# Giving two of GpSimd's one-operation instructions a second operation (a multiplication by one)

## The chip, the core and the metric

The kernel runs on one core of one Trainium2 chip. The metric is the device time of one execution in microseconds. Engines are called as the profile calls them: PE is TensorE's matmul, PEld its weight load, DVE is VectorE, ACT is ScalarE, POOL is GpSimd, SP is SyncE, which here only issues transfers.

## The reference

One layer of an encoder over 1024 positions of width 1024, all in float32. Cut to what this change touches:

```python
def rmsnorm(x, w):
    y = x * lax.rsqrt(jnp.mean(x * x, axis=-1, keepdims=True) + EPS)
    return y * w
...
h = rmsnorm(x, norm_mix_w) * (1 + sc_m) + sh_m
z, xbc, dt_raw, q, k, v = jnp.split(h @ w_in, IN_SPLITS, axis=-1)
y_ssd = ssd_mixer(z, xbc, dt_raw, ...)            # a scan over chunks, with an rmsnorm at its end
# attention: 8 heads of 64, each chunk of 64 positions sees itself and 8 chunks before it
scores = einsum(q, k) * 64 ** -0.5
p = softmax(where(valid, scores + bias, min), axis=-1)
y_att = einsum(p, v)
x = x + g_m * (concat([y_ssd, y_att]) @ w_out)
x = x + g_f * conv_ffn(rmsnorm(x, norm_ffn_w) * (1 + sc_f) + sh_f)
return rmsnorm(x, final_norm_w)
```

## The kernel before

**Stages.** The kernel first norms x and multiplies it into the first two pairs of heads' q, k and v (0 to about 102 us in the trace), then does attention (about 102 to 312 us, mingled with the projections that come next), the scan and the projection to x (to about 600 us), and the feed-forward part (from there to the end). Float32 products are made from a high and a low part, three matmuls for one (lines 76 to 78); `split` makes the two parts (lines 85 and 86).

**Attention.** The eight heads go in four pairs `p`, each pair in four units `u`, each unit in two rows of 128 queries (`i` = 2u and 2u + 1) and two heads `h`. `attn_scores` does one `i`: PE writes scores of up to 640 keys into PSUM (line 262); DVE adds the bias, negates and takes the minimum over the row (line 413); ACT takes the exponential and the row sum (line 416); DVE inverts the sum (line 418); POOL scales the row in place by it (line 419, one operand a column of one number per partition). The tile is `p`, of which there are eight buffers. `attn_pv` then transposes each scaled tile in blocks of 128 on PE, ACT and DVE split the result, and PE multiplies it with v:

```python
                if c0 == 0:
                    T.transpose(tps[:, o:o + P], p0[:, (j - lo0) * P:(j - lo0 + 1) * P], ident)   # line 445
                ...
                    T.transpose(tps[:, o1:o1 + P], p1[:, (j - lo1) * P:(j - lo1 + 1) * P], ident) # line 448
            split(hi, lo, tps[:, 0:used], A, V)
            ...
                T.matmul(pv[:, c0:c0 + n], w, hi[:, o:o + n], start=g == 0, stop=False)           # line 456
```

Between the units stand other products: the q, k and v of the later pairs (`gemm_part`, into PSUM tiles named `acc`), and beside the last pair the first projection of the scan (tiles named `s`, lines 76 to 78). For PE they are filling: they need nothing from attention. POOL also makes the low part of some weights there (line 86, `wl`), and blanks two corners of each bias tile (lines 475 and 476).

**The norms.** `rstd` takes a mean of squares, adds epsilon on POOL (line 116) and raises it to the power of minus one half on POOL (line 117). It runs 16 times on one column: 8 times in the first stage, 8 times in the scan. The norms at the end use another function (line 931), which the change leaves alone.

**What sets the order.** Nothing in these stages is ordered by hand but for a few places. The framework schedules the whole program when it is built: it reckons a duration for each instruction, and by these sets the order of instructions on every engine and of transfers on SP's queue. Each engine then runs its own list in that order, so an instruction that is not ready holds up all behind it on its engine. A change of one instruction's reckoned duration can so move instructions on every engine.

Of the kernel before, what the change touches and what calls it, by code (L numbers as in the profile page):

```python
# [13 lines left out]
ALU = mybir.AluOpType  # L14
# [50 lines left out]
def tile_block(ctx: ExitStack, tc: tile.TileContext, x, crep, pk, w_ada, w_first, w_ft, w_z,  # L65
# [3 lines left out]
    G = nc.gpsimd  # L69
# [36 lines left out]
    def stat(n=1):  # L106
        if stc[0] + n > 64:
            stc[0] = 0
        a = st1[:, stc[0]:stc[0] + n]
        stc[0] += n  # L110
        return a

    def rstd(ms, eps=EPS):
        n = ms.shape[-1]
        r = stat(n)
        G.tensor_scalar(ms, ms, eps, None, op0=ALU.add)
        G.tensor_tensor(r, ms, mhalf[:, 0:n], ALU.pow)
        return r

# [132 lines left out]
    def scores(p, i):  # L252
        d = qk[p]
        j0 = max(0, i - 4)
        n = (i - j0 + 1) * P
        off = (j0 - (i - 4)) * P
        parts = [(0, n)] if n <= 512 else [(0, 320), (320, 320)]
        st = [s_tile(), s_tile()]
        for h in range(2):
            for pi, (a, w) in enumerate(parts):  # L260
                for ti, kn in enumerate(("kh", "kl")):
                    T.matmul(st[h][:, 512 * pi:512 * pi + w], d["q"][h][:, i * P:(i + 1) * P],
                             d[kn][h][:, j0 * P + a:j0 * P + a + w], start=ti == 0, stop=ti == 1)
        return st, n, off, parts
# [31 lines left out]
    def norm1(st):  # L296
        ms = stat()
        junk = s0.tile([P, D], F32, tag="junk", name="junk")
        norm_to(xts[st], junk, ms)
        r = rstd(ms)  # L300
        V.tensor_scalar(xts[st], xts[st], r, None, op0=ALU.mult)
# [93 lines left out]
    def p_tile():  # L395
        return pp.tile([P, 640], F32, tag="p", name="p")
# [4 lines left out]
    def attn_scores(p, i, bt):  # L401
        st, n, off, parts = s00 if p + i == 0 else scores(p, i)
        res = []
        for h in range(2):
            pt_ = p_tile()
            nm, rs = stat(), stat()
            if len(parts) == 1:
                src, bsl, dst = st[h][:, 0:n], bt[h][:, off:off + n], pt_[:, 0:n]
            else:
                src = st[h].rearrange("p (a b) -> p a b", a=2)[:, :, 0:320]  # L410
                bsl = bt[h].rearrange("p (a b) -> p a b", a=2)
                dst = pt_.rearrange("p (a b) -> p a b", a=2)
            V.tensor_tensor_reduce(out=dst, in0=src, in1=bsl, scale=-1.0, scalar=3e38,  # L413
                                   op0=ALU.add, op1=ALU.min, accum_out=nm)
            pv_ = pt_[:, 0:n]
            A.activation(pv_, pv_, AF.Exp, scale=-1.0, bias=nm, accum_out=rs)
            rr = stat()
            last_v[:] = [V.reciprocal(rr, rs).ins]  # L418
            G.tensor_scalar(pv_, pv_, rr, None, op0=ALU.mult)  # L419
            res.append(pt_)  # L420
        return res

# [46 lines left out]
    def attention(p, extra=()):  # L469
        extra = dict(extra)  # L470
        bt = []
        for h in range(2):
            t = bp.tile([P, 640], F32, tag="bias", name="bias")
            nc.sync.dma_start(t, bias[2 * p + h])
            G.memset(t[0:64, 576:640], -1e30)
            G.memset(t[64:128, 0:64], -1e30)
            bt.append(t)
        for u in range(4):
            pa = attn_scores(p, 2 * u, bt)
            pb = attn_scores(p, 2 * u + 1, bt)  # L480
            for fn in extra.get(u, ()):
                fn()
            if p == 3:
                if u < 2:
                    early[4 + 2 * u] = wu_pair(w_ft[4 + 2 * u], A, G)
                for _ in range(MODS[u]):
                    mod_col(todo.pop(0), mtq[len(todo) % 4], last_v[0])
            for h in range(2):
                attn_pv(p, u, h, pa[h], pb[h])
# [345 lines left out]
    def ssd_norm(c, y, t, at=None):  # L835
        with tc.issue_after(at) if at else ExitStack():
            V.tensor_tensor(y, y, zs[:, c, 0:512], ALU.mult)
        ms = stat()
        A.activation(t, y, AF.Square, accum_out=ms)
        r = rstd(ms, 512.0 * EPS)  # L840
        A.activation(y, y, AF.Copy, scale=r)
# [724 lines left out]
```

## Time and profile before

| | us |
|---|---|
| median of 3 runs (1219.9 to 1223.88) | 1221.77 |
| the profiled execution | 1219.7 |
| its span, first to last instruction | 1217.7 |
| PE busy | 1167.9 |
| DVE busy | 927.8 |
| ACT busy | 597.0 |
| POOL busy | 199.9 |
| POOL's scaling, line 419, 64 instructions | 98.8 |
| POOL's epsilon, line 116, 16 instructions | 6.8 |

The mean clock granted to PE is 0.994. Busy PE is not PE at its peak, since matmuls overlap and their ends are modelled. Idle time of an engine is put down to what ended it. The numbers of the trace come from one execution, whose time outside the span is 2.0 us.

### The profile page before, as it was taken

How to read it: one execution, taken by the hardware profiler on the slowest of the kernel's cores; microseconds unless marked ns; L12 is line 12 of the kernel's file. 1: busy time of each engine (PE TensorE's matmuls, PEld its weight loads, DVE VectorE, ACT ScalarE, POOL GpSimd, SP SyncE). 2: the span in 40 equal slices, each digit the busy share in tenths (PEclk: the TensorE clock that was granted, in tenths of full speed). 3: DMA queues.
4: the chain of work that ended last, by engine and by line, in shares of the span. 5: the costliest groups of instructions: out<-in, count | busy, mean ns of one | idle time of the engine just before them, and what ended most of it. 6: DMA issues, size and time to landing. Idle time of an engine off the chain costs nothing.

```text
span 1217.7 us, 15636 instructions
## 1 busy us (share of the span) xinstructions
PE 1167.9 (96%) x5802; PEld 974.4 (80%) x5802; DVE 927.8 (76%) x1394; ACT 597.0 (49%) x1001; POOL 199.9 (16%) x174
## 2 busy tenths in 40 slices
PE   4998899989999989999999999999999999999996
PEld 3877787878878978888878888888888888888885
DVE  6846454686597678746999988988889869756986
ACT  4536454674243666676644533344334445433444
POOL 1205563672000034300000000000000000000522
PEclk9999999999999999999999999999999999999998
DMA  9722211311477201141123223322232278733443
GB/s 334 256 58 64 65 56 46 102 66 52 152 248 241 88 13 40 53 150 58 70 95 112 104 95 130 124 77 85 104 130 98 83 277 278 266 120 130 149 137 146
DMA packets 56395, 150.86 MB, mean 124 GB/s; under 512 B 5632, under 2 KB 5760, under 8 KB 54912
## 3 DMA queue, kind: packets, MB, share of 16 engines
q1 hardware_dynamic: 49264, 125.49, 30.6%
q10 hardware_dynamic: 7056, 24.38, 5.0%
q8 instruction: 45, 0.74, 0.3%
q14 instruction: 30, 0.25, 0.1%
HBM read 116.56 MB, written 29.10 MB: 120 GB/s over the span
## 4 chain that ended last, share of the span: by engine, by line
PE 80%; DVE 10%; ACT 4%; DMA 2%; issue 2%; POOL 1%; SPq 0%; POOLq 0%; DVEq 0%; ACTq 0%
PE wops L699 5%; PE dn L78 5%; PE dn L76 5%; PE dn L77 5%; PE uY L76 5%; PE uY L78 5%; PE uY L77 4%; PE uX L78 3%; PE uX L76 3%; PE uZ L77 3%; PE uX L77 3%; PE uZ L76 3%; PE uZ L78 3%; PE s L76 3%; PE s L77 2%; PE s L78 2%
## 5 line engine op out<-in xcount | busy, mean ns | idle before, releaser
L1427 POOL TENSOR_TENSOR ya<-ya,xs 128x512 f32<-128x512 f32 x4 | 17.2, 4334 | 557.7 <-ACT xs L1423 557.7
L77 PE MATMUL dn<-w 128*128 128x512 f32 x296 | 108.1, 392 | 0.0
L76 PE MATMUL dn<-w 128*128 128x512 f32 x296 | 108.1, 391 | 0.0
L419 POOL TENSOR_SCALAR p<-p,st 128x640 f32<-128x640 f32 (+4 forms) x64 | 98.8, 1558 | 43.9 <-DVE st L418 36.6
L78 PE MATMUL dn<-w 128*128 128x512 f32 x296 | 100.2, 391 | 0.2 <-DVE w L86 0.2
L76 PE MATMUL uY<-tH,w 128*128 128x512 f32 x248 | 97.2, 392 | 0.0
L77 PE MATMUL uY<-tL,w 128*128 128x512 f32 x248 | 97.0, 391 | 0.0
L78 PE MATMUL uY<-tH,w 128*128 128x512 f32 x248 | 96.9, 391 | 0.0
L85 ACT ACTIVATE w<-ya 128x1024 fp32r<-128x1024 f32 (+1 forms) x41 | 39.2, 956 | 87.5 <-PE uY L78 84.2
L699 PE MATMUL wops<-hH,yhl 128*128 128x512 f32 x224 | 74.1, 399 | 2.9 <-DVE yhl L86 1.5
L78 PEld LDWEIGHTS dn<-w 128*128 128x128 f32 x296 | 55.4, 188 | 13.3 <-DVE w L86 1.1
L76 PEld LDWEIGHTS dn<-w 128*128 128x128 f32 x296 | 55.5, 188 | 12.3
L77 PEld LDWEIGHTS dn<-w 128*128 128x128 f32 x296 | 55.5, 188 | 12.2
L85 ACT ACTIVATE w<-xs 128x1024 fp32r<-128x1024 f32 (+1 forms) x41 | 39.1, 954 | 37.3 <-PE uY L78 33.3
L78 PEld LDWEIGHTS uY<-tH,w 128*128 128x128 f32 x248 | 46.5, 188 | 10.4
L76 PEld LDWEIGHTS uY<-tH,w 128*128 128x128 f32 x248 | 46.6, 188 | 10.3
L77 PEld LDWEIGHTS uY<-tL,w 128*128 128x128 f32 x248 | 46.6, 188 | 10.2
L413 DVE CUSTOM_DVE_ANT_0 p<-s,bias 128x640 f32<-128x640 f32 (+4 forms) x64 | 40.4, 651 | 17.0 <-PE tp L445 5.2
L76 PE MATMUL s<-hH,wh 128*128 128x512 f32 x128 | 50.1, 391 | 2.4 <-DVE ct L520 2.3
L86 DVE TENSOR_TENSOR pt<-tp,pt 128x512 fp32r<-128x512 f32 (+2 forms) x72 | 41.5, 595 | 13.2 <-ACT pt L85 12.8
L699 PEld LDWEIGHTS wops<-hH,yhl 128*128 128x128 f32 x224 | 41.8, 188 | 12.2 <-DVE yhl L86 1.9
L1101 DVE SCALAR_TENSOR_TENSOR a<-cv,pkt,a 128x1023 f32<-128x1023 f32 (+1 forms) x40 | 51.1, 1279 | 0.1
(459 smaller groups left out, 3428.8 us busy)
## 6 DMA issues: line engine op xcount, KB each, us to landing
wos<-in_w_ada_dram SPq DMA_DIRECT2D x25, 512.0 KB, 4.6
gz<-a ACTq DMA_DIRECT2D x10, 1024.0 KB, 5.0
ya<-in_w_up_dram SPq DMA_DIRECT2D x11, 768.0 KB, 4.2
xs<-in_w_up_dram SPq DMA_DIRECT2D x11, 768.0 KB, 4.3
adat<-in_w_ada_dram SPq DMA_DIRECT2D x16, 512.0 KB, 5.5
raws<-in_w_ft_dram SPq DMA_DIRECT2D x14, 512.0 KB, 4.2
gy<-a ACTq DMA_DIRECT2D x10, 512.0 KB, 2.6
qk<-in_x_dram SPq DMA_DIRECT2D x8, 512.0 KB, 6.6
```

Source lines behind the costliest of these rows:

```text
L76: T.matmul(ps, lh, rh, start=start, stop=False, skip_group_check=more)
L77: T.matmul(ps, lh, rl, start=False, stop=False, skip_group_check=more)
L78: T.matmul(ps, ll, rh, start=False, stop=stop, skip_group_check=more)
L85: i = A.activation(hi, src, AF.Copy) if ehi is A else ehi.tensor_copy(hi, src)
L86: return i, elo.tensor_tensor(lo, src, f32(hi), ALU.subtract)
L413: V.tensor_tensor_reduce(out=dst, in0=src, in1=bsl, scale=-1.0, scalar=3e38, op0=ALU.add, op1=ALU.min, accum_out=nm)
L419: G.tensor_scalar(pv_, pv_, rr, None, op0=ALU.mult)
L699: i = op(*a, **k)
L1101: V.scalar_tensor_tensor(a[:, j:S], c[:, 0:S - j], w[2 - j], a[:, j:S], op0=ALU.mult, op1=ALU.add)
L1427: G.tensor_tensor(src, src, fnr[:, halves[1]], ALU.mult)
```

## The change

Both POOL instructions get a second operation, a multiplication by 1.0, in the same instruction. The values stay the same, and no instruction is added or removed.

```diff
     def rstd(ms, eps=EPS):
         n = ms.shape[-1]
         r = stat(n)
-        G.tensor_scalar(ms, ms, eps, None, op0=ALU.add)
+        G.tensor_scalar(ms, ms, eps, 1.0, op0=ALU.add, op1=ALU.mult)
         G.tensor_tensor(r, ms, mhalf[:, 0:n], ALU.pow)
         return r
...
             rr = stat()
             last_v[:] = [V.reciprocal(rr, rs).ins]
-            G.tensor_scalar(pv_, pv_, rr, None, op0=ALU.mult)
+            G.tensor_scalar(pv_, pv_, rr, 1.0, op0=ALU.mult, op1=ALU.mult)
             res.append(pt_)
```

It also moves instructions, since the scheduler reckons another duration for these two. Up to the start of attention all engines' lists are as before; from the first scaled tiles on PE's list differs in 39 places up to the scan, and is the same again after that.

The first place on PE is in pair 0, unit 0. `p_935` and `p_940` are the scaled tiles of the second row of queries, one for each head; `s_989` and `s_990` are scores of unit 1, `s_1055` of unit 2.

```order
 L262 MATMUL s_989<-qk_136,qk_134 128x512
 L262 MATMUL s_989<-qk_138,qk_134 128x512
+L448 MATMUL tp_946<-ident_69,p_935 128x128 x2
 L262 MATMUL s_990<-qk_137,qk_135 128x512
 L262 MATMUL s_990<-qk_139,qk_135 128x512
-L448 MATMUL tp_946<-ident_69,p_935 128x128 x2
+L448 MATMUL tp_960<-ident_69,p_940 128x128 x2
 L262 MATMUL s_1055<-qk_136,qk_134 128x320
 L262 MATMUL s_1055<-qk_138,qk_134 128x320
 L262 MATMUL s_1055<-qk_136,qk_134 128x320
 L262 MATMUL s_1055<-qk_138,qk_134 128x320
-L448 MATMUL tp_960<-ident_69,p_940 128x128 x2
```

The transposes of both scaled tiles now stand ahead of scores that they stood behind.

The second place on PE is later in pair 0: `p_1065` and `p_1085` are the first head's two tiles of unit 2, `acc_1327` is a projection for pair 2 and so filling. Before, this stood behind the last transposes of unit 1:

```order
L448 MATMUL tp_1042<-ident_69,p_1000 128x128 x2
L76 MATMUL acc_1327<-hH1_84,wh_1322 128x512
L77 MATMUL acc_1327<-hL1_86,wh_1322 128x512
L78 MATMUL acc_1327<-hH1_84,wl_1323 128x512
L76 MATMUL acc_1327<-hH1_84,wh_1322 128x512
L77 MATMUL acc_1327<-hL1_86,wh_1322 128x512
```

In the changed kernel, behind the last product of unit 1's first head:

```order
L457 MATMUL pv_1005<-pt_910,v_122 128x128
L445 MATMUL tp_1096<-ident_69,p_1065 128x128
L448 MATMUL tp_1096<-ident_69,p_1085 128x128
L445 MATMUL tp_1096<-ident_69,p_1065 128x128
L448 MATMUL tp_1096<-ident_69,p_1085 128x128
L262 MATMUL s_1283<-qk_142,qk_140 128x128
L262 MATMUL s_1283<-qk_144,qk_140 128x128
L262 MATMUL s_1284<-qk_143,qk_141 128x128
L262 MATMUL s_1284<-qk_145,qk_141 128x128
L76 MATMUL acc_1327<-hH1_84,wh_1322 128x512
```

What stands ahead of these transposes is the same set of instructions as stood ahead of `acc_1327` before. The transposes of unit 2, which stood behind 22 matmuls of filling, and the scores of pair 1 now stand ahead of the filling.

On POOL the first difference is at the end of pair 0 and the start of pair 1 (the rows of 128x128 are pair 1's first):

```order
 L419 TENSOR_SCALAR p<-p,st_72 128x512 x2
-L419 TENSOR_SCALAR p<-p,st_72 128x640 x6
+L419 TENSOR_SCALAR p<-p,st_72 128x640 x5
+L475 MEMSET bias 64x64
+L419 TENSOR_SCALAR p<-p,st_72 128x640
+L476 MEMSET bias 64x64
+L475 MEMSET bias 64x64
+L419 TENSOR_SCALAR p<-p,st_72 128x640
+L476 MEMSET bias 64x64
+L419 TENSOR_SCALAR p<-p,st_72 128x640
+L419 TENSOR_SCALAR p<-p,st_72 128x128
+L86 TENSOR_TENSOR wl<-raws,wh 128x1024
```

The blanking of bias corners, and with it the transfers that fill those tiles, stands a few scalings earlier, and one scaling of pair 1 ahead of the weights' low part. The order of the scalings among themselves is unchanged. On SP's queue two stretches of loads (bias and weights in attention; adaptive-scale and output weights after it) are interleaved in another order.

## The prediction

> **What bounds the kernel now.** I read the page first, for who is busy.
>
> ```profile
> span 1217.7 us, 15636 instructions
> PE 1167.9 (96%) x5802; PEld 974.4 (80%) x5802; DVE 927.8 (76%) x1394; ACT 597.0 (49%) x1001; POOL 199.9 (16%) x174
> L419 POOL TENSOR_SCALAR p<-p,st 128x640 f32<-128x640 f32 (+4 forms) x64 | 98.8, 1558 | 43.9 <-DVE st L418 36.6
> ```
>
> PE is busy for 96% of the span. POOL, whose instructions change, is busy for 16%, and half of that (98.8 us) is the scaling of the probabilities. The next question is who waits for this scaling. The view of line 419 answers it, and the view of PE's waits between 60 and 275 us says what PE waits for there instead.
>
> ```profile
> who waited for it (us, times):
>   PEld tp L445: 1.1, 2
>   PE tp L445: 0.7, 1
> PE s L262 <- DVE st L413: 4.2, 10, 1.1
> ```
>
> In the whole span PE waits 0.7 us for a scaled tile and its weight load 1.1 us. PE's largest wait in attention, 4.2 us, is for DVE's row minimum, which frees the PSUM of the scores. So the scaling is not on the path that sets the end. But an average hides where POOL is full, so I read stretches of 10 us (columns: stretch, length, then busy time of PE, PEld, DVE, ACT, POOL, the granted clock, the share of DMA, GB/s), and POOL's timeline.
>
> ```profile
> 100.00:110.00 10.00, 8.61 (x43) 6.58 (x42) 5.35 (x24) 5.13 (x17) 5.59 (x12) 1.00 0.23 84
> 110.00:120.00 10.00, 8.20 (x56) 6.93 (x54) 8.51 (x27) 9.16 (x23) 10.00 (x7) 1.00 0.00 1
> 120.00:130.00 10.00, 8.49 (x47) 7.20 (x48) 5.22 (x14) 6.08 (x12) 9.71 (x10) 1.00 0.20 66
> 250.00:260.00 10.00, 9.19 (x64) 7.85 (x64) 9.46 (x33) 8.43 (x25) 6.19 (x6) 1.00 0.00 0
> 260.00:270.00 10.00, 8.37 (x53) 7.00 (x54) 9.88 (x28) 7.97 (x20) 9.73 (x6) 1.00 0.29 94
> 107.39 17.62 POOL L419 TENSOR_SCALAR p<-p,st 128x256 f32<-128x256 f32 x11 [0.60 <-DVE st L418]
> 125.38 3.75 POOL L419 TENSOR_SCALAR p<-p,st 128x640 f32<-128x640 f32 x2
> 262.72 18.94 POOL L419 TENSOR_SCALAR p<-p,st 128x640 f32<-128x640 f32 x8 [0.27 <-DVE st L418]
> ```
>
> In pair 0, from 107.39 to 129.13 us, POOL scales without a gap; in pair 3, from 262.72 to 281.66, again. These are the places where the price of a scaling can matter: in these five stretches PE is idle for 1.39 + 1.80 + 1.51 + 0.81 + 1.63 = 7.1 us. In the pairs between them POOL has gaps.
>
> **The price of the second operation.** No instruction of the trace of before has it, so I bound it by the nearest rows, POOL's groups kept apart by shape (busy us, then mean ns of one).
>
> ```profile
> L419 POOL TENSOR_SCALAR p<-p,st 128x640 f32<-128x640 f32 x32 | 63.8, 2010 | 6.0 <-DVE st L418 5.2 <-PE pv L457 0.8
> L419 POOL TENSOR_SCALAR p<-p,st 128x384 f32<-128x384 f32 x8 | 9.9, 1246 | 9.1 <-DVE st L418 7.8 <-PE tp L448 1.3
> L419 POOL TENSOR_SCALAR p<-p,st 128x128 f32<-128x128 f32 x8 | 4.8, 608 | 12.5 <-DVE st L418 7.3 <-PE acc L78 4.9
> L708 POOL TENSOR_TENSOR xdd<-xdt,ex 128x512 f32<-128x512 f32 x8 | 8.8, 1100 | 156.2 <-ACT ex L687 128.7 <-PE stp L699 22.3 <-DVE xdt L707 5.2
> L116 POOL TENSOR_SCALAR st<-st x16: 213/281/1289, 7.4 to 516.0; 128x1 f32<-128x1 f32 x16
> ```
>
> From 128 to 384 columns the scaling grows by 638 ns, so 2.49 ns a column, beside a fixed 608 − 128 × 2.49 = 289 ns. All 64 scalings have 30,720 columns (eight each of 128, 256, 384 and 512, and 32 of 640). The upper bound is that the second multiplication costs a column as much as the first, 4.98 ns: 640 columns would take 3.48 us, and all scalings 30,720 × 4.98 ns + 64 × 0.289 us = 171 us. The lower bound lies below today's price, since another elementwise multiplication on the same engine is cheaper although it reads two tiles: (1100 − 289) / 512 = 1.58 ns a column. A scaling on such a path would take 1.30 us for 640 columns, all of them 67 us. I take today's price: the nearest row is the same instruction with the same operands and the same column of numbers, and only the arithmetic in it grows. Both ends stay for the range.
>
> [...]
>
> **Epsilon.** Undisturbed, the addition at line 116 takes 213 ns for one column. Should a second operation cost as much as the whole instruction, 16 × 0.213 = 3.4 us would be added if every one of them were on the path. Most of them are under PE's work, so I take nothing and bound it by −1 to +2 us.
>
> **The moved instructions.** The scheduler's new list puts transposes of scaled tiles earlier on PE, ahead of scores and of filling. Each transpose that isn't ready holds all behind it. For pair 0 this can be worked out from rows.
>
> ```profile
> 106.80 1.20 PE L262 MATMUL s<-qk 128*128 128x512 f32 x4 [0.30 <-DVE st L413]
> 119.95 0.51 PE L76 MATMUL acc<-hH,wh 128*128 128x512 f32 x1
> 126.97 0.29 PE L448 MATMUL tp<-ident,p 128*128 128x128 f32 x1
> ```
>
> First place: p_940 is the first of the 11 scalings that start at 107.39. With 0.289 + 256 × 2.49 ns = 0.93 us it is done at 108.32, while PE ends the scores s_990 at 108.00. PE would wait about 0.3 us where it didn't before, with s_1055 queued behind it; but that score had a wait of its own of about this size for DVE's minimum, so most of it is not lost.
>
> Second place: before, PE reaches acc_1327 at 119.95, and transposes p_1085 only at 126.97. Now that transpose comes ahead of the filling, with the same instructions ahead of it, so about 119.95. The run of 11 scalings ends at 125.01 and p_1085 is the fourth from its end, so with 1.875 us each (3.75 / 2) it is ready at 125.01 − 3 × 1.875 = 119.4. At today's price the new order just fits: margin 0.55 us. It would not have to fit at a higher price, which is a rival below.
>
> Of PE's 39 changed places most are such exchanges of independent work, with all PE work unchanged. Moved loads on SP: the bias tiles come earlier, and after attention the only wait that a weight load ends on PE is small:
>
> ```profile
> PE s L76 <- DVE ct L520: 2.3, 1, 2.3
> ```
>
> Behind this is DVE's reduction of loaded weights; I bound the new interleaving by ±2.3 us and take nothing.
>
> **The sum.** Waits for the scaling that could go: at most 0.7 + 1.1 us. New waits where transposes now come just in time: 0.3 us at the first place, and a few like it, about 1 us. Epsilon 0, loads 0. Together about −0.5 us, on the profiled execution 1219.2 us. That execution's 1219.7 us stands 2.1 us below the median of 1221.77, so against the median the forecast is 1221.3 us: no change. A measurement of this kernel can tell about 0.3%, 3.7 us, from no change.
>
> **Rivals.** *The scaling gets cheaper, and the order was right for it: faster.* On the lower price pair 0 needs 7680 × (2.49 − 1.58) ns = 7.0 us less of POOL, and so does pair 3, so the two full stretches thin out. For it: the multiplication with two inputs is cheaper today, and the new order reads as that of a scheduler which reckons the scaled tiles ready sooner. Against: PE's waits there name DVE, not POOL, and the reckoning is no evidence for the chip. The most it can bring is PE's idle 7.1 us in those stretches; taking 5 of them gives 1216.8 us.
>
> *The price stays and the order is worse: slower.* The margin at the second place is 0.55 us, and if the chain of scores, minimum, exponential and inverse runs a little later in the new order, transposes wait with filling behind them. With 0.3 us at 20 to 39 of the changed places this is +6 to +12 us; I take +7, 1229 us. For it: an order reckoned for another price than the chip's. Against: PE's filling is the same, and only its place moves.
>
> *The second operation costs a column as much as the first: slower, and by more.* This is one mechanism at one place, POOL's run in pair 0. From 107.39 to the end of p_1085 it scales 256 + 2 × 384 + 2 × 512 + 3 × 640 = 3968 columns; 2.49 ns more for each makes 9.9 us, so p_1085 is ready at 129.3 instead of 119.4. In the old order its transpose at 126.97 would have waited 2.3 us. In the new one PE stands from 119.95 to 129.3, 9.3 us, with the filling queued behind the transpose. It decides as soon as the price rises by more than 0.55 us over these 3968 columns, 0.14 ns a column. If the three other pairs pay half of it each, it is 9.3 + 3 × 4.7 = 23 us: 1245 us; 9 to 37 us are its bounds. Against it: only the arithmetic doubles, not the reads and writes.
>
> [...]
>
> That the change does nothing, because a multiplication by one is dropped on the way, is part of the first case for the price, but the order of instructions would still be the new one.
>
> **How the numbers follow.** No change 0.35; cheaper scaling 0.27; worse order 0.23; dearer scaling 0.15. So faster by over 0.3% has 0.27, within it 0.35, slower 0.23 + 0.15 = 0.38. The time is that of the likeliest, 1221.3 us; its own range is 1218 to 1225. The range of 1212 to 1239 us leaves out the upper half of the dearer scaling (0.10), and some 0.05 each of a gain beyond 7.1 us with better order, and of a worse order with other losses.
>
> **What would show it.** In the profile of the changed kernel, the group of line 419 with 128x640: near 2.0 us says that the second operation is free, near 1.3 us or 3.5 us names the other two cases. In pair 0, the transposes at about 120 us without a wait for POOL confirm the second place; a wait of PE at line 445 or 448 for POOL's p of several us speaks for the dearer scaling, and many short ones for the worse order. PE idle between 100 and 130 us well below 4.7 us speaks for the cheaper one. The forecast is wrong if PE's waits for p grow beyond 4 us in total, if the end of attention moves by more than 3.7 us, or if the difference comes from behind attention, where I expect none.

## The result, and the profile after

The changed kernel takes 1217.04 us, median of 7 runs (1213.17 to 1219.3), against 1221.77 us for 7 runs of the kernel before (1219.9 to 1223.88). The ratio is 0.9963, with a 95% interval of 0.9947 to 0.9979. That is 0.37% faster, just beyond the 0.3% that the prediction takes as what a measurement can tell from no change (the seven runs of before spread over 0.33%). The forecast of no change, 1221.3 us with a range of its own of 1218 to 1225, was not the case that happened, though the time is inside the whole range of 1212 to 1239 us; the rival of the cheaper scaling gave 1216.8 us.

The page of the changed kernel, and POOL's groups by shape (busy us, then mean ns of one):

```profile
span 1217.5 us, 15642 instructions
PE 1170.7 (96%) x5802; PEld 977.2 (80%) x5802; DVE 928.7 (76%) x1394; ACT 598.1 (49%) x1001; POOL 148.6 (12%) x174
L419 POOL TENSOR_SCALAR p<-p,st 128x640 f32<-128x640 f32 (+4 forms) x64 | 46.1, 726 | 76.7 <-DVE st L418 66.5
...
L419 POOL TENSOR_SCALAR p<-p,st 128x640 f32<-128x640 f32 x32 | 28.3, 891 | 21.7 <-DVE st L418 19.4 <-PE pv L456 1.5 <-PE s L262 0.6
L419 POOL TENSOR_SCALAR p<-p,st 128x384 f32<-128x384 f32 x8 | 4.7, 588 | 17.2 <-DVE st L418 17.2
L419 POOL TENSOR_SCALAR p<-p,st 128x128 f32<-128x128 f32 x8 | 3.0, 374 | 10.7 <-DVE st L418 10.6
```

With the second operation the scaling takes less than half: 0.89 us for 640 columns where it was 2.01, and 46.1 us in all where it was 98.8. From 128 to 384 columns it grows by 214 ns, 0.84 ns a column. POOL now waits 66.5 us for DVE's inverse (line 418) before scalings, and in the next view PE waits for it 1.1 us at the longest. What PE waits for between 95 and 330 us (in total, times, longest):

```profile
PE acc L76 <- DVE qk L232: 3.4, 4, 1.1
PE acc L76 <- DVE qk L239: 2.2, 4, 1.1
PE tp L445 <- POOL p L419: 1.8, 2, 1.1
PE s L262 <- DVE st L413: 1.6, 5, 0.5
```

The wait for the scaled tile did not go; it grew from 0.7 to 1.8 us. What went is more than half of the wait for DVE's row minimum, from 4.2 to 1.6 us, although DVE has the same instructions as before, only in another order. So the gain is not in the wait that belongs to the cheaper instruction.

The profiled execution of the changed kernel happens to be the longest of its seven (1219.3 us) and had a mean granted clock of 0.991 where that of before had 0.994. For comparisons of traces the experiment with the scaling alone, below, serves better: it has the same order of instructions on every engine as the changed kernel, and its profiled execution had 0.996. That execution is the other extreme, though: at 1214.58 us it is the shortest of its 12 (median 1217.27), and the mean clock of the 12 is 0.9936. Beside the trace of before, which is near its median, it shows more gain than there is in the medians.

### The profile page after: what moved, and what is told of

Same layout as the page of the kernel before. It is cut to its first block, busy times and chain, and to the rows that moved or that the text cites. A ratio compares the mean times of both kernels' runs of the same rounds, so it can differ in the third digit from the quotient of the medians.

```text
span 1217.5 us, 15642 instructions
## 1 busy us (share of the span) xinstructions
PE 1170.7 (96%) x5802; PEld 977.2 (80%) x5802; DVE 928.7 (76%) x1394; ACT 598.1 (49%) x1001; POOL 148.6 (12%) x174
## 4 chain that ended last, share of the span: by engine, by line
PE 70%; DVE 5%; ACT 1%; issue 1%; DMA 1%; POOL 0%; POOLq 0%; DVEq 0%; ACTq 0%; SPq 0%
PE wops L699 6%; PE dn L78 5%; PE dn L77 5%; PE dn L76 5%; PE uY L76 5%; PE uY L78 5%; PE uY L77 4%; PE uX L78 3%; PE uX L76 3%; PE uZ L77 3%; PE uZ L76 3%; PE uX L77 3%; PE uZ L78 3%; PE s L76 3%; PE s L77 3%; PE s L78 3%
## 5 line engine op out<-in xcount | busy, mean ns | idle before, releaser
L78 PEld LDWEIGHTS dn<-w 128*128 128x128 f32 x296 | 55.4, 188 | 13.2 <-DVE w L86 1.1
L419 POOL TENSOR_SCALAR p<-p,st 128x640 f32<-128x640 f32 (+4 forms) x64 | 46.1, 726 | 76.7 <-DVE st L418 66.5
```

The source lines that it names most:

```text
L78: T.matmul(ps, ll, rh, start=False, stop=stop, skip_group_check=more)
L419: G.tensor_scalar(pv_, pv_, rr, 1.0, op0=ALU.mult, op1=ALU.mult)
```

## The experiments

Two questions stand. What does the second operation cost, and for which instructions? And does the time come from the price, from the order, or from both together? For the second question the two were taken apart: a kernel can be held to the order of another by giving each engine the other's list of instructions, as edges that order the issue and wait for nothing. Two kernels held so have, on every engine and on SP's queue, exactly the order of the one that they were held to. No kernel was run held to its own order. But the traces show that the holding adds no instruction: 15,636 are recorded for before and for the kernel held to it, and 15,642 for after and for the two held to it. (The six more that the new order has are all for semaphores.)

**The price by itself.** A kernel of POOL's instructions alone, one behind the other, on 128 and 640 columns, with the column of numbers as in line 419 or with constants:

```diff
+    put(lambda n: G.tensor_scalar(tl(n, 'mult_col'), tl(n, 'mult_col'), c, None, op0=M))
+    put(lambda n: G.tensor_scalar(tl(n, 'mult_col_mult'), tl(n, 'mult_col_mult'), c, 1.0, op0=M, op1=M))
+    put(lambda n: G.tensor_scalar(tl(n, 'mult_col_min'), tl(n, 'mult_col_min'), c, 3e38, op0=M, op1=MN))
...
+    put(lambda n: G.tensor_scalar(tl(n, 'mult_imm_mult'), tl(n, 'mult_imm_mult'), 1.0, 1.0, op0=M, op1=M))
```

> This kernel computes nothing of the layer: it copies a tile of x to the output and runs GpSimd's tensor_scalar alone, in twelve forms, on tiles of 128 and 640 columns, three times each, with no other engine beside it, and a two-input multiplication and a copy for comparison. Theory 1 (any second arithmetic operation takes the cheap path): all two-operation forms take about 0.37 us for 128 columns and 0.80 us for 640, all one-operation forms about 0.60 and 1.88 us, whether the operand is a column or a constant. Rival 2 (only some pairs of operations are cheap): multiplication with multiplication or addition is near 0.80 us, and pairs with minimum or subtraction are near or above 1.88 us. Rival 3 (it is the operands: a column with a constant is cheap): the form with two columns and the forms with constants alone differ from the column with a constant at the same operations.

Some of POOL's groups by shape; each tile is named after the operations on it:

```profile
L128 POOL TENSOR_SCALAR mult_col_sub<-mult_col_sub,col 128x640 f32<-128x640 f32 x3 | 7.3, 2423 | 0.3
L127 POOL TENSOR_SCALAR mult_col_min<-mult_col_min,col 128x640 f32<-128x640 f32 x3 | 7.3, 2419 | 0.3
L122 POOL TENSOR_SCALAR mult_col<-mult_col,col 128x640 f32<-128x640 f32 x3 | 5.6, 1882 | 0.3
L129 POOL TENSOR_SCALAR mult_imm<-mult_imm 128x640 f32<-128x640 f32 x3 | 5.4, 1807 | 0.2
L135 POOL TENSOR_TENSOR tt<-tt,src 128x640 f32<-128x640 f32 x3 | 4.6, 1530 | 0.2
L124 POOL TENSOR_SCALAR mult_col_add<-mult_col_add,col 128x640 f32<-128x640 f32 x3 | 2.4, 799 | 0.3
L123 POOL TENSOR_SCALAR mult_col_mult<-mult_col_mult,col 128x640 f32<-128x640 f32 x3 | 2.4, 798 | 0.3
L130 POOL TENSOR_SCALAR mult_imm_mult<-mult_imm_mult 128x640 f32<-128x640 f32 x3 | 2.2, 724 | 0.2
L137 POOL COPY cp<-src 128x640 f32<-128x640 f32 x3 | 2.2, 721 | 0.2
...
L127 POOL TENSOR_SCALAR mult_col_min<-mult_col_min,col 128x128 f32<-128x128 f32 x3 | 2.1, 710 | 0.3
L122 POOL TENSOR_SCALAR mult_col<-mult_col,col 128x128 f32<-128x128 f32 x3 | 1.8, 599 | 0.2
L123 POOL TENSOR_SCALAR mult_col_mult<-mult_col_mult,col 128x128 f32<-128x128 f32 x3 | 1.1, 372 | 0.2
```

A multiplication followed by a multiplication or an addition takes 798 ns for 640 columns, and one multiplication alone takes 1882 ns. A column costs (798 − 372) / 512 = 0.83 ns in the pair and (1882 − 599) / 512 = 2.51 ns in the single one; with constants the pair is as fast as a copy (724 and 721 ns). It is neither any second operation (with a minimum or a subtraction as the second, 3.3 ns a column, dearer than none) nor the column of numbers (one multiplication by a constant is slow too, 1807 ns). So among the forms that were run, the fast one belongs to certain pairs of operations. Per column the single multiplication takes three times as long as the pair with a multiplication (2.51 ns beside 0.83), and the pair with a minimum four times (3.3 ns).

**Each half of the change alone.** Epsilon alone, and the scaling alone:

```diff
-        G.tensor_scalar(ms, ms, eps, None, op0=ALU.add)
+        G.tensor_scalar(ms, ms, eps, 1.0, op0=ALU.add, op1=ALU.mult)
```

> Only the addition of epsilon gets the second operation. Its list of instructions has the same order on every engine as before. Theory 1 (epsilon plays no part): ratio to before 1.000, inside 0.998 to 1.002, and the line of epsilon takes about 0.2 us undisturbed as before. Rival (epsilon brings part of the gain): ratio 0.997 to 0.998.

```diff
-            G.tensor_scalar(pv_, pv_, rr, None, op0=ALU.mult)
+            G.tensor_scalar(pv_, pv_, rr, 1.0, op0=ALU.mult, op1=ALU.mult)
```

> Only the scaling of the probabilities gets the second operation. Its list of instructions has the same order on every engine as the fully changed kernel. Theory 1: the whole effect is here, ratio to before 0.996 (0.994 to 0.998), scaling of 640 columns 0.80 us undisturbed. Rival (epsilon brings part): ratio 0.998 to 1.000.

Epsilon alone: 1220.13 us (12 runs) beside 1220.68 us (23 runs of before), ratio 1.0003 (0.9988 to 1.0018); it leaves the order as it was. The scaling alone: 1217.27 us (12 runs), ratio 0.9969 (0.9956 to 0.9982); it has the whole order of the changed kernel, and the whole of its gain.

**The price without the order, and the order without the price.** First the changed kernel held to the order of before, then the kernel before held to the order of after (one line for each; `ORDER` lists the instructions of the other kernel for each engine):

```diff
+        for a, b in zip(ns, ns[1:]):
+            tc.add_manual_dep(traced[b], a, info, reason="order")
```

> Both second operations are in (scaling of 640 columns 0.80 us), but every engine and queue is held to the order of the kernel before. Theory P (the price alone makes the gain): ratio to before 0.996 to 0.9975. Theory O (the new order alone makes it): 0.999 to 1.001. Theory PO (a cheaper scaling pays only where the order lets PE take the tiles sooner): 0.998 to 1.000, and PE's waits for DVE's row minimum stay near 4 us.

> No second operation (scaling of 640 columns 1.88 us), but every engine and queue is held to the order of the changed kernel. Theory P: ratio to before 0.999 to 1.002. Theory O: 0.996 to 0.998. Theory PO, and the prediction's rival of the worse order: 1.002 to 1.008, with PE's waits for the scaled tiles at lines 445 and 448 of 4 to 10 us; by the prediction's working the transposes at the second place of pair 0 (near 120 us) just fit, without a wait of more than 0.5 us.

| price of 640 columns | order of before | order of after |
|---|---|---|
| 2.01 us, one operation | 1 (the kernel before) | 1.0036 (1.0018 to 1.0053), 1223.61 us |
| 0.89 us, the pair | 1.0003 (0.9992 to 1.0015), 1221.29 us | 0.9969 (0.9956 to 0.9982), scaling alone |

The runs of before beside the held kernels had a median of 1220.2 us. The cheaper scaling by itself brings nothing that can be measured, and the new order by itself costs 0.36%, part of it by the clock (below). Only together do they gain 0.3 to 0.4%. PE's waits between 95 and 330 us with the cheap scaling in the old order:

```profile
PE s L262 <- DVE st L413: 4.9, 10, 1.4
PE tp L445 <- POOL p L419: 0.7, 1, 0.7
```

These are the waits of before (4.2 us in 10 and 0.7 us in 1). In this order the transposes stand late enough for the dear scaling, so a tile that is ready sooner is not used sooner, and the scores meet DVE's minimum as early as ever. With the old price in the new order, the same view, and then two rows of PE's timeline (start, length, instruction, and in brackets the idle time before it and what ended it):

```profile
PE s L262 <- DVE st L413: 2.8, 5, 1.6
PE tp L448 <- POOL p L419: 1.9, 3, 1.0
```

```profile
107.57 0.44 PE L448 MATMUL tp<-ident,p 128*128 128x128 f32 x2 [0.16 <-DVE st L418]
...
111.56 0.33 PE L448 MATMUL tp<-ident,p 128*128 128x128 f32 x1 [0.95 <-POOL p L419]
118.69 0.33 PE L448 MATMUL tp<-ident,p 128*128 128x128 f32 x1 [0.21 <-POOL p L419]
```

The new order does shorten the wait for the minimum, from 10 times to 5. That this is because transposes now stand between scores is read from the lists and was not tested apart; DVE's own list is another one too. At the old price it is paid for with waits for POOL: these 1.9 us and 0.7 us at line 445, 2.6 us in all. That is less than the 4 to 10 us that were expected, and with the cheap price in the same order it is 1.8 us.

**A dearer scaling in the new order.** The pair with a minimum, which the first experiment found dearer, in the order of after. It measures what the third rival was about.

```diff
-            G.tensor_scalar(pv_, pv_, rr, None, op0=ALU.mult)
+            G.tensor_scalar(pv_, pv_, rr, 3e38, op0=ALU.mult, op1=ALU.min)
```

> The scaling's second operation is a minimum with 3e38, which changes no value and takes 2.42 us for 640 columns by the run of the forms; every engine and queue is held to the order of the changed kernel. The price is 0.54 us above the one of before, so the theory that a late scaling holds up PE in this order (PO, and the prediction's dearer scaling) expects 3 to 12 us more than the kernel with the old price in the new order: ratio to before 1.004 to 1.015, with a wait of about 1 to 2 us at the second place of pair 0. Theory O expects 0.996 to 0.999 also here.

It takes 1231.0 us (4 runs), ratio 1.0092 (1.0078 to 1.0105). The group of the scalings, PE's waits, and the second place in PE's timeline:

```profile
L419 POOL TENSOR_SCALAR p<-p,st 128x640 f32<-128x640 f32 x32 | 79.0, 2483 | 1.7 <-DVE st L418 1.5
```

```profile
PE tp L448 <- POOL p L419: 5.0, 4, 2.2
PE s L262 <- DVE st L413: 3.9, 4, 3.2
```

```profile
122.63 0.33 PE L448 MATMUL tp<-ident,p 128*128 128x128 f32 x1 [2.25 <-POOL p L419]
```

The wait of 3.2 us for the minimum is POOL's as well. DVE waits there for the blanking of a bias tile's corner (line 475), which stands on POOL's list behind four scalings:

```profile
240.87 9.61 POOL L419 TENSOR_SCALAR p<-p,st 128x640 f32<-128x640 f32 x4 [0.33 <-DVE st L418]
250.60 0.29 DVE L413 CUSTOM_DVE_ANT_0 p<-s,bias 128x128 f32<-128x128 f32 x1 [4.42 <-POOL bias L475]
```

At the old price in the same order these four scalings take 7.46 us, DVE waits 2.54 us for the blanking, and PE waits 1.65 us for DVE, the longest of its five such waits above. In the trace of the changed kernel neither DVE nor PE waits there. So the dear scaling reaches PE in two ways: by the tile itself (2.25 us at the second place), and by what stands behind it on POOL (3.2 us).

So with the order fixed the price matters at every step: 0.89, 2.01 and 2.48 us for 640 columns give 0.9969, 1.0036 and 1.0092.

These waits add up to less than the time: some 9 us here, and only part of them is new. Much of the rest is in the granted clock. The following rows are stretches from 97 us to PE's last transpose of a scaled tile, one for each kernel: before, scaling alone, old price in the new order, dearer price (columns as in the prediction; the last but two is the granted clock):

```profile
97.00:311.80 214.80, 200.22 (x1162) 170.82 (x1161) 128.18 (x336) 119.50 (x270) 116.08 (x89) 0.99 0.20 61
```

```profile
97.00:310.00 213.00, 199.76 (x1170) 170.95 (x1169) 131.01 (x339) 122.16 (x272) 64.16 (x89) 1.00 0.20 61
```

```profile
97.00:315.30 218.30, 201.68 (x1165) 171.67 (x1164) 131.22 (x339) 122.16 (x272) 116.50 (x89) 0.99 0.19 59
```

```profile
97.00:324.30 227.30, 208.62 (x1171) 178.43 (x1170) 132.18 (x339) 122.16 (x272) 139.82 (x89) 0.95 0.19 58
```

PE's idle time is 14.6, 13.2, 16.6 and 18.7 us. With the dearer price PE is also busy for 8.9 us longer than with the cheap one over the same matmuls, at a clock of 0.95. Over all runs of a kernel the mean granted clock is 0.9936 for the changed kernel and 0.9936 to 0.9939 for before, 0.9904 for the old price in the new order, and 0.9858 for the dearer one. Reckoned on the whole span, the last two would lose (0.9936 − 0.9904) × 1219 = 3.9 of their 4.2 us and 9.5 of their 11.0 us (of the mean spans) in this way. That is too much, as runs of equal clock show. Three runs of the old price in the new order had a clock of 0.993 or 0.994 and take 1222.2 us on average; 17 such runs of before take 1220.1 us. So about 2.1 us of the loss stay at equal clock, as much as PE's idle time in attention grows (from 14.6 to 16.6 us), and about half of it is clock.

In the trace of the dearer price the clock falls in attention, to 0.95, beside these waits. For the old price in the new order it is not shown that waits in attention lower it. Its clock in attention is that of before, 0.99. What its trace loses more lies in the scan, where PE's list is that of before, and the trace of epsilon alone, in the old order and at the old price, loses as much there (288.3 and 288.8 us from PE's last transpose of a scaled tile to the first product of the stage after the scan, 286.3 in before). From 420 to 460 us before has a granted clock of 0.96; these two rows are the old price in the new order and epsilon alone:

```profile
420.00:460.00 40.00, 35.33 (x183) 30.58 (x182) 27.93 (x38) 26.58 (x64) 11.10 (x11) 0.83 0.06 20
```

```profile
420.00:460.00 40.00, 35.45 (x180) 30.58 (x178) 27.72 (x41) 24.29 (x62) 10.52 (x12) 0.83 0.08 27
```

Two of its eight runs, with a clock of 0.985, make up more than half of the difference in its mean clock, and where those lose it was not traced. The gain of the changed kernel is not of this kind: its clock is that of before.

**One step further.** POOL is now idle for longer in attention (busy 64.2 us of it with the scaling alone, 116.1 in before), so I gave it the low parts of the scan's weights, which DVE makes:

```diff
-        wh, wl = early.pop(ft) if ft in early else wu_pair(w_ft[ft], A, V)
+        wh, wl = early.pop(ft) if ft in early else wu_pair(w_ft[ft], A, G)
```

> The changed kernel, with the low parts of the scan's projection weights (six subtractions of 128x1024 beside and behind the last pair) made on GpSimd instead of VectorE, since the cheaper scaling leaves GpSimd free there. If VectorE's work holds up PE near the end of attention, ratio to before 0.993 to 0.996. If PE's filling hides it anyway: 0.995 to 0.998, the same as the changed kernel. A subtraction takes 2.4 us on GpSimd against 1.1 us on VectorE, so where a low part is waited for it gets slower: up to 1.000.

It takes 1220.73 us (11 runs), ratio to before 1.0003 (0.9994 to 1.0012), so the gain is gone. A subtraction takes 2.40 us on POOL and 1.22 us on DVE in the trace of before (line 86, `wl`), where the expectation has 2.4 and 1.1. This edit, too, changes the order that the scheduler makes, and the two effects were not taken apart here. The changed kernel is the fastest that was run.

## Why the prediction was right or wrong

**What bounds the kernel: right, and read too narrowly.** PE's path did not have the scaling on it: with the order held, 53 us less of POOL's work bring nothing. But I concluded that a cheaper scaling could gain little because PE's waits name DVE. The waits that shrank are those for DVE. As I read the lists, an order that can use the tile sooner puts transposes between scores, and DVE gets time for the minimum. So a wait that the trace puts down to DVE was shortened (from 4.2 to 1.6 us) by a change on POOL alone, with the order that goes with it; and DVE itself waits for POOL, as it did for 4.42 us for the blanking with the dearer scaling.

**The price of the second operation: the step that failed.** I bounded a column between 1.58 and 4.98 ns and took 2.49. It is 0.84, below the lower bound: all scalings take 46.1 us, where the bound gave 67 and the value taken 95 (30,720 × 2.49 ns and 64 × 0.289 us; the trace of before has 98.8). Nothing in the trace of before showed a fast form: the nearest row, a single multiplication, had 2.49. That a pair would be cheaper than one operation alone was not among my reasons; the rival had it by the wrong mechanism, a price like that of two input tiles (1530 ns for 640 columns in the run of the forms, where the pair takes 798).

**Epsilon: right.** Taken as 0, bounded by −1 and +2 us, measured at a ratio of 1.0003.

**The first place: right, and of no weight.** At the old price I gave the transposes of the second row of queries a wait of 0.3 us. In the trace of that case they begin at 107.57 us after 0.16 us of waiting, put down to DVE's inverse. At the new price there is none.

**The second place: right.** I worked out that p_1085 just fits at the old price, with a margin of 0.55 us, and would wait up to 9.3 us at twice the price. At the old price it comes 0.21 us late, at 118.69; at 2.48 us a tile it waits 2.25; and in the changed kernel it comes without a wait, as PE's timeline has it:

```profile
118.62 0.30 PE L445 MATMUL tp<-ident,p 128*128 128x128 f32 x1
118.75 0.27 PE L448 MATMUL tp<-ident,p 128*128 128x128 f32 x1
```

The wait of 0.95 us at 111.56, some 7 us earlier, I had not worked out.

**The rivals.** *Cheaper scaling and the order right for it* is what happened: −5 us was forecast, the medians differ by 4.7, and by 3.4 for the scaling alone beside its 23 runs of before. That 1216.8 us is so near is in good part luck, since the price was taken at nearly twice what it is and the account holds in part. The account was that PE's idle 7.1 us in the five full stretches thins out. In the trace of the scaling alone these stretches are idle for 1.37 + 1.54 + 0 + 1.39 + 1.14 = 5.4 us:

```profile
100.00:110.00 10.00, 8.63 (x46) 6.83 (x45) 6.00 (x27) 5.93 (x20) 3.92 (x13) 1.00 0.15 54
110.00:120.00 10.00, 8.46 (x58) 7.17 (x57) 9.83 (x30) 9.77 (x23) 5.15 (x7) 1.00 0.14 40
120.00:130.00 10.00, 10.00 (x62) 8.59 (x61) 4.03 (x14) 5.50 (x14) 4.30 (x9) 1.00 0.07 28
250.00:260.00 10.00, 8.61 (x59) 7.19 (x58) 9.65 (x26) 7.84 (x20) 3.67 (x5) 1.00 0.16 52
260.00:270.00 10.00, 8.86 (x53) 7.44 (x52) 9.41 (x27) 6.48 (x16) 6.46 (x7) 1.00 0.18 54
```

So 1.7 us of the 5 are there. I also named 100 to 130 us, with 4.7 us idle, as the place to look; 2.9 are left. The rest shows up later. The first product of the stage after the scan, uY, comes at 598.1 us in before and at 593.2 with the scaling alone (line 76 by tile: count, shortest, median and longest ns, first and last start):

```profile
L76 PE MATMUL uY<-tH,w x248: 387/392/398, 598.1 to 989.5; 128*128 128x512 f32 x124
```

```profile
L76 PE MATMUL uY<-tH,w x248: 387/392/398, 593.2 to 984.7; 128*128 128x512 f32 x124
```

From there to the last of these products the two take the same time, so all of the difference lies ahead of it. The end of attention (311.8 and 310.0 us) has only 1.8 of these 4.9 us, and nearly all of these 1.8 are one stretch at about half clock that of these two only the trace of before has (238 to 245 us, shown at the end; by an estimate from the granted clock 4.00 × 0.07 + 3.00 × 0.48 = 1.7 us). But by then PE has also done 8 more matmuls in that stretch (x1170 against x1162): filling has been drawn forward, and the time for it is saved later. One wait behind attention is smaller as well, in the view of PE's waits from 312 to 600 us, scaling alone:

```profile
PE s L76 <- DVE ct L520: 0.7, 1, 0.7
```

It was 2.3 us, and 1.6 in the changed kernel's own trace. I had bounded it and taken nothing. But it is 1.2 us with the cheap price in the old order, which gains nothing, so it is not shown to belong to the gain. How the gain divides beyond these terms (14.58 − 13.24 = 1.3 us of idle in attention, up to 0.7 to 1.6 us here) stays open. In the changed kernel's own trace, at a clock of 0.991, uY comes at 598.0 us, no earlier than before. That a difference would come from behind attention was one of the marks that I gave for being wrong. It is met in so far as most of the 4.9 us shows up there.

*Price stays, order worse*: +7 us was forecast, from many short waits. The chip gives +3.4 us in the medians, and not by many waits: there are three for p at line 448 and one for the minimum behind POOL's blanking, and about half of the loss is clock. *The second operation costs as much as the first*: 1245 us was for 3.48 us a tile; 2.48 us a tile gave 1231.0. The forecast's mechanism, the wait at the second place, was there with 2.25 us, and neither the blanking nor the clock was in it. Two multiplications on one element take 0.83 ns a column and one alone 2.51, so the second added no cost.

**The sum.** −0.5 us was the sum of terms on a price that did not hold. Price and order were set down as separate terms, and they are not: the cheap price is worth nothing measurable in the old order and about 0.7% in the new one (about 0.4% at equal clock, 1217.5 us for four runs of the scaling alone at 0.993 or 0.994 against 1222.2). That the time came out inside the range was not the price being right: the price was off by a factor of three, and in the old order it would have changed nothing.

## What to carry to other kernels

Where a scheduler orders the work by durations that it reckons, a cheaper instruction is worth what the new order makes of it: here the same price had a ratio of 1.0003 in the old order and 0.9969 in the new one. Read the chain of waits for what stands in a fixed order, and test price and order apart by holding the order. Before a price is taken from the nearest row, measure the form itself: here one more operation took an instruction of 640 columns from 1882 to 798 ns. Follow a wait one engine further: the engine that it names may itself be waiting, as DVE was for POOL's blanking (4.42 us). Read the granted clock beside PE's waits: with the dearer scaling it was 0.95 in attention, and PE was busy for 8.9 us longer over the same matmuls than with the cheap one, beside some 9 us of waits.

## What the runs showed of the hardware

GpSimd's multiplication by a column takes 0.83 ns a column in a pair with a multiplication or addition, 2.51 ns alone and 3.3 ns in a pair with a minimum (run of the forms). I had not expected that less work could take three times as long.

The clock granted to PE fell to about half behind short waits of PE in two places, to 0.52 in the kernel before, at the start of pair 3, and to 0.50 with the dearer scaling, a little later (stretches with the granted clock last but two):

```profile
238.00:242.00 4.00, 2.61 (x16) 1.92 (x16) 3.36 (x10) 3.98 (x10) 3.67 (x3) 0.93 0.91 340
242.00:245.00 3.00, 3.00 (x16) 3.00 (x16) 1.54 (x5) 0.90 (x5) 3.00 (x3) 0.52 1.03 404
```

```profile
247.00:250.00 3.00, 0.76 (x8) 0.52 (x6) 0.00 (x0) 0.47 (x1) 3.00 (x2) 0.97 0.28 108
250.00:256.00 6.00, 4.95 (x20) 4.45 (x21) 3.29 (x13) 2.94 (x9) 4.00 (x7) 0.50 0.00 0
```

Four microseconds with PE busy for 65% are followed by three at a clock of 0.52, and a wait of 3.2 us for DVE's minimum by six at 0.50. In the first place PE's longest single wait is 0.79 us. A stretch like it also passed without a drop: the scaling alone has 2.53 us busy between 236 and 240 us, with a longest wait of 0.80 us, and keeps a clock of 1.00 there and in the ten microseconds behind. What decides between the two was not tried.
